# A gated short-convolution layer on one core: the adaLN sums divided anew between TensorE, VectorE and ScalarE, wider late groups, and products ordered by channel tile

## The chip, the core and the metric

The kernel runs on one core of one Trainium2 chip. A core has a TensorE (PE, the matmuls; its weight loads are listed apart as PEld), a VectorE (DVE), a ScalarE (ACT), a GpSimd (POOL) and a SyncE (SP) that here issues nearly all DMAs. Time is device microseconds (us) of one execution. Before the change the median of three runs is 928.99 us (926.72 to 929.95).

## The reference

One layer (DEPTH = 1, so the short convolution alone), 256 tokens of 2048 channels, all float32:

```python
h = rmsnorm(x, norm_g)                          # over the 2048 channels of a token
mod = silu(c) @ ada_w + ada_b                   # adaLN: one vector, 2048 -> 3 * 2048
shift, scale, gate = split(mod, 3)
h = h * (1 + scale) + shift
b_gate, c_gate, v, g = split(h @ w_in, 4)       # w_in: 2048 x 16384
u = causal_depthwise_conv(c_gate * v, conv_w)   # 3 taps
y = (b_gate * u * silu(g)) @ w_out              # w_out: 4096 x 2048
out = rmsnorm(x + gate * y, final_g)
```

## The kernel before

**Products in three terms.** Each float32 operand is split into a rounded high part and a remainder. `split` makes them of a weight tile: ACT casts `raw` to `hi` (L320), DVE subtracts to get `lo` (L321). The activations are kept turned, channel by token, in `hT`: for each of the 16 tiles of 128 input channels ("plane" k) the high part `hh_` and the remainder `hl_`. `product` (L415) issues hi·hh, hi·hl and lo·hh, each a matmul of 128x128 by 128x256.

**First half of the channels (`mm_s`).** A chunk is 512 channels of one quarter of `w_in`; 4 chunks by 4 quarters are kept as 16 accumulators `acc`. adaLN's shift and scale become known group by group of planes (`ADA = [2] * 8`: eight groups of two), and a product can use a plane only when its group is done. So `plan` walks through the 16 accumulators several times: `part` multiplies the planes k0 to k1 that are there by then, into a PSUM bank, and `keep` adds it to `acc` (L436, L438) or the bank is seeded from `acc` (L448). `plan` has figures of its own for what each step takes (`VPIECE`, `ALAG`) and puts the DMAs of adaLN's weights (`ada_piece`, L384, two DMAs for each tile `at`) between the parts. 24 products (two planes) come of 512 KB of `w_in`.

**adaLN's sums.** For a group, DVE accumulates silu(c)[k] times a row block of `ada_w` into `gv` (L395, L397): 16 row tiles, each 512 wide (256 of shift, 256 of scale). That leaves 128 partial sums, one per partition. `ada_done` turns `gv` on PE (L404, 4 transposes into PSUM `tp_g`), ACT sums each of the four blocks (L406, with an accumulator read), and `modulate` adds the biases on DVE (L305 to L307), writes `hh_` on ACT (L310), then shift and remainder on DVE (L311, L314). The first group has no time to wait: its 16 row tiles `at0` are the first thing loaded after x; DVE takes 13 of them (L344, L346), PE takes tiles 7, 11 and 15 directly as matmuls with silu(c) as the moving column (`sum0`, L333), and at the end PE adds DVE's partial sums by a column of ones. Between these, `idle` issues transposes into an unused bank (L236).

**Second half (`mm_b`).** Here all planes are there: banks of 256 channels, all 16 planes, per channel tile 8 planes times 3 terms in a row. The gate's part of adaLN (`gate_sums`, tiles `at_g` of 512 KB, four groups of 512) has the lowest priority; each group ends with matmuls by ones (`ps_gate`, L538).

**Last product (`mm_o`).** `w_out` in four column blocks, then gate, residual and the last rmsnorm.

**What sets the order.** Up to the first group's end the order on each engine is the order of the code (`in_order`). After that the framework's scheduler orders each engine's instructions by its own model; `later(GIVE)` lets adaLN's sums go behind other work. Every engine runs its list strictly in that order. Buffers: `raw` 3, `hi` 3, `lo` 3, `at` 4, PSUM `mm` 3, PSUM `sm` 2.

Of the kernel before, what the change touches and what calls it, by code (L numbers as in the profile page):

```python
# [13 lines left out]
P = 128  # L14
# [10 lines left out]
CT = 4  # L25
NCH = 4
NS = CT * NCH
ADA = [2] * 8
# [12 lines left out]
VPIECE = 1.5  # L41
# [5 lines left out]
ALAG = 9.0  # L47
# [4 lines left out]
def plan():  # L52
# [10 lines left out]
    def ada():  # L63
        nonlocal load, dve
        k0, nk, i = pieces.pop(0)
        steps.append(("ada", k0, nk, i))
        load = max(load, dve - AAHEAD) + ALOAD
        dve = max(dve, load + 2.0) + VPIECE
        if i == 4 * nk - 1:
            ready.extend([dve + ALAG] * nk)  # L70

# [46 lines left out]
def short_conv_layer(ctx: ExitStack, tc: tile.TileContext, x, c, norm_g, ada_w, ada_b, w_in, conv_w, w_out, final_g, out):  # L118
# [6 lines left out]
    const = ctx.enter_context(tc.tile_pool(name="const", bufs=1))  # L125
    adap = ctx.enter_context(tc.tile_pool(name="adap", bufs=2))
# [59 lines left out]
    IDLE = (16, 30, 24, 14, 14, 6)  # L186
# [58 lines left out]
    gT = vec[:, 0:16]  # L245
    b_shift = vec[:, 16:32]
    b_scale1 = const.tile([P, KT], F32, tag="bsc", name="b_scale1")
# [17 lines left out]
    nc.vector.tensor_scalar_add(b_scale1, vec[:, 32:48], 1.0)  # L265
# [11 lines left out]
    def turn_x(k0, k1, vector=False):  # L277
# [8 lines left out]
        for i in range(0, k1 - k0, 2):  # L286
# [4 lines left out]
            nc.scalar.copy(xs[k0 // CT][:, k0 % CT + i : k0 % CT + i + 2, :], tp)  # L291

    shift = const.tile([P, KT], F32, tag="shift", name="shift")
    scale = const.tile([P, KT], F32, tag="scale", name="scale")

    def modulate(k0, nk, sums):

        ks = slice(k0, k0 + nk)
        if nk == 1:
            nc.vector.tensor_scalar(  # L300
                out=scale[:, ks], in0=sums[1], scalar1=b_scale1[:, ks], scalar2=gT[:, ks], op0=ALU.add, op1=ALU.mult
            )
            nc.scalar.activation(shift[:, ks], sums[0], AF.Identity, bias=b_shift[:, ks])
        else:
            nc.vector.tensor_tensor(out=scale[:, ks], in0=sums[1], in1=b_scale1[:, ks], op=ALU.add)  # L305
            nc.vector.tensor_tensor(out=scale[:, ks], in0=scale[:, ks], in1=gT[:, ks], op=ALU.mult)
            nc.vector.tensor_tensor(out=shift[:, ks], in0=sums[0], in1=b_shift[:, ks], op=ALU.add)  # L307
        for k in range(k0, k0 + nk):
            hf = xs[k // CT][:, k % CT, :]
            nc.scalar.activation(hh_[:, k], hf, AF.Identity, bias=shift[:, k : k + 1], scale=scale[:, k : k + 1])  # L310
            nc.vector.tensor_scalar(  # L311
                out=hf, in0=hf, scalar1=scale[:, k : k + 1], scalar2=shift[:, k : k + 1], op0=ALU.mult, op1=ALU.add
# [3 lines left out]
    def split(raw, n):  # L316

        hi = wpool.tile([P, SLOT], F32R, tag="hi", name="hi", bufs=3)
        lo = wpool.tile([P, SLOT], F32R, tag="lo", name="lo", bufs=3)
        nc.scalar.copy(hi[:, :n], raw[:, :n])  # L320
        nc.vector.tensor_tensor(out=lo[:, :n], in0=raw[:, :n], in1=hi[:, :n].bitcast(F32), op=ALU.subtract)  # L321
        return hi, lo


    ON_PE = (7, 11, 15)
    sums0 = psum.tile([P, 512], F32, tag="sm", name="sum0", bufs=2)
    gv0 = adap.tile([P, 2, 2 * P], F32, tag="gv", name="gv0")[:, :, 0 : NK0 * P]
    turn_x(0, 4)

    def sum0(k, rows, col):  # L330

        for o in range(2 * NK0):
            nc.tensor.matmul(  # L333
                sums0[:, o : o + 1], rows[:, o // NK0, (o % NK0) * P : (o % NK0 + 1) * P], col,
                start=k == ON_PE[0] and o == 0, stop=k is None, skip_group_check=True,
            )

    for k in range(KT):
        c_k = silu_c[:, k : k + 1]
        if k in ON_PE:  # L340
            idle(IDLE[2 + ON_PE.index(k)])
            sum0(k, first_ada[k], c_k)
        elif k == 0:
            nc.vector.tensor_scalar_mul(gv0, first_ada[k], c_k)  # L344
        else:
            nc.vector.scalar_tensor_tensor(out=gv0, in0=first_ada[k], scalar=c_k, in1=gv0, op0=ALU.mult, op1=ALU.add)  # L346
    sum0(None, gv0, ones[:, 0:1])
    pieces0 = [split(raw0[:, 0 : CT * P], CT * P)]
    modulate(0, NK0, (sums0[:, 0:NK0], sums0[:, NK0 : 2 * NK0]))
    idle(IDLE[-1])  # L350
    pinned.close()
    with behind(ended):
        for k in range(1, NK0):
            pieces0.append(split(raw0[:, k * CT * P : (k + 1) * CT * P], CT * P))
# [345 lines left out]
```

## Time and profile before

| | |
|---|---|
| median of three runs | 928.99 us |
| the profiled execution's own time | 927.38 us |
| its span, first to last instruction | 925.6 us |
| first product of the trunk | 26.32 us |
| `mm_s` / `mm_b` / `mm_o` begin | 26.3 / 393.9 / 742.9 us |
| PE busy in the span | 906.1 us (98%) |
| DVE / ACT busy | 613.8 us (66%) / 472.9 us (51%) |
| DMA | 227.66 MB, mean 246 GB/s |

"Start" times are from the span's first instruction. A matmul's end is modelled, so the distance between starts tells PE's rate, not the length of one. A few matmul records are missing from the trace. In a row of stretches, the number in parentheses behind an engine is its count of instructions, PEclk is the granted share of TensorE's clock.

### The profile page before, as it was taken

To read this page: it belongs to the slowest core of one execution; us is meant where nothing else is said; L and a number is where in the kernel's file an instruction comes from. 1 tells how busy PE (TensorE), PEld (TensorE's weight loads), DVE (VectorE), ACT (ScalarE), POOL (GpSimd) and SP (SyncE) were. 2 spreads that over 40 slices of the span, in tenths; PEclk is the share of its full clock that TensorE was granted. 3 is DMA by queue.
4 is the path that set the end of the run, shared out by engine and by line. 5 is a ranking of instruction groups with operands and counts; after the bars stand their busy time and mean duration, and the time that the engine had idled before them with its cause. 6 is when DMAs were issued, how large, how long until landed. Compare 5 with 4: busy or idle time off the path is not lost.

```text
span 925.6 us, 16468 instructions
## 1 busy us (share of the span) xinstructions
PE 906.1 (98%) x7119; PEld 871.4 (94%) x7119; DVE 613.8 (66%) x604; ACT 472.9 (51%) x465; POOL 0.7 (0%) x6
## 2 busy tenths in 40 slices
PE   6999999999999999999999999999999999999996
PEld 6999999999999999999999999999999988888885
DVE  5889988897585799875554455445554554545882
ACT  3787866765557756644334433443334433444333
POOL 0000000000000000000000000000000000000000
PEclk9999999999999999999999999999999999999999
DMA  9999999999885689776656665666556685565542
GB/s 314 362 365 354 369 367 350 338 364 350 273 293 164 221 294 356 238 233 201 203 184 190 200 202 183 191 200 201 183 183 197 206 324 184 183 203 203 182 137 91
DMA packets 163753, 227.66 MB, mean 246 GB/s; under 512 B 5680, under 2 KB 104160, under 8 KB 163296
## 3 DMA queue, kind: packets, MB, share of 16 engines
q1 hardware_dynamic: 163440, 226.51, 73.4%
q8 instruction: 56, 0.92, 0.4%
q10 hardware_dynamic: 240, 0.09, 0.0%
q14 instruction: 17, 0.14, 0.0%
HBM read 224.49 MB, written 2.10 MB: 245 GB/s over the span
## 4 chain that ended last, share of the span: by engine, by line
PE 88%; DMA 5%; DVE 3%; ACT 1%; issue 1%; SPq 0%; ACTq 0%; DVEq 0%
PE mm_b L415 38%; PE mm_s L415 31%; PE mm_o L601 6%; PE mm_o L599 6%; PE mm_o L600 6%; DMA at<-in_ada_w_dram 2%; DMA raw_s<-in_sc_w_in_dram 2%; DVE gv L397 1%; DVE lo L321 1%; ACT hi L320 1%; DMA x<-in_x_dram 1%; PE ps_gate L538 0%; PE sum L333 0%; ACT x L281 0%; ACT x L285 0%
## 5 line engine op out<-in xcount | busy, mean ns | idle before, releaser
L415 PE MATMUL mm_s<-hT,hi 128*128 128x256 f32 x2048 | 355.0, 279 | 0.4 <-ACT hT L310 0.3
L415 PE MATMUL mm_b<-hT,hi 128*128 128x256 f32 x2048 | 348.8, 276 | 0.0
L415 PEld LDWEIGHTS mm_s<-hT,hi 128*128 128x128 f32 x2048 | 310.9, 189 | 1.4 <-ACT hT L310 0.7
L415 PEld LDWEIGHTS mm_b<-hT,hi 128*128 128x128 f32 x2048 | 308.7, 188 | 0.2 <-issue 0.2
L415 PE MATMUL mm_s<-hT,lo 128*128 128x256 f32 x1024 | 285.0, 279 | 4.6 <-DVE lo L321 4.6
L415 PE MATMUL mm_b<-hT,lo 128*128 128x256 f32 x1024 | 282.6, 276 | 0.0
L321 DVE TENSOR_TENSOR lo<-raw,hi 128x2048 fp32r<-128x2048 f32 (+1 forms) x66 | 148.1, 2244 | 134.9 <-ACT hi L320 134.9
L320 ACT CAST hi<-raw 128x2048 fp32r<-128x2048 f32 (+1 forms) x66 | 123.7, 1875 | 208.4 <-PE mm_b L415 150.1
L415 PEld LDWEIGHTS mm_s<-hT,lo 128*128 128x128 f32 x1024 | 192.3, 188 | 5.4 <-DVE lo L321 5.4
L415 PEld LDWEIGHTS mm_b<-hT,lo 128*128 128x128 f32 x1024 | 192.2, 188 | 0.2 <-issue 0.2
L321 DVE TENSOR_TENSOR lo<-raw_s,hi 128x2048 fp32r<-128x2048 f32 (+1 forms) x80 | 147.9, 1849 | 43.9 <-ACT hi L320 43.2
L320 ACT CAST hi<-raw_s 128x2048 fp32r<-128x2048 f32 (+1 forms) x80 | 124.7, 1558 | 69.6 <-PE mm_s L415 57.8
L321 DVE TENSOR_TENSOR lo<-raw_o,hi 128x2048 fp32r<-128x2048 f32 x32 | 73.3, 2291 | 65.8 <-ACT hi L320 65.8
L320 ACT CAST hi<-raw_o 128x2048 fp32r<-128x2048 f32 x32 | 61.3, 1915 | 107.0 <-PE mm_o L601 89.7
L600 PE MATMUL mm_o<-lo,y 128*128 128x512 f32 x256 | 99.7, 391 | 0.0
L599 PE MATMUL mm_o<-hi,y 128*128 128x512 f32 x256 | 99.3, 389 | 0.0
L601 PE MATMUL mm_o<-hi,y 128*128 128x512 f32 x256 | 99.3, 389 | 0.0
L397 DVE SCALAR_TENSOR_TENSOR gv<-at,silu_c,gv 128x512 f32<-128x512 f32 x105 | 78.6, 750 | 5.8 <-DMA at<-in_ada_w_dram 4.4
L436 ACT COPY acc<-mm_s 128x1024 f32<-128x1024 f32 x54 | 54.4, 1010 | 32.3 <-PE mm_s L415 32.3
L600 PEld LDWEIGHTS mm_o<-lo,y 128*128 128x128 f32 x256 | 48.1, 188 | 10.2 <-issue 0.2
L601 PEld LDWEIGHTS mm_o<-hi,y 128*128 128x128 f32 x256 | 48.1, 188 | 10.2 <-issue 0.2
L599 PEld LDWEIGHTS mm_o<-hi,y 128*128 128x128 f32 x256 | 48.1, 188 | 9.9
(94 smaller groups left out, 375.2 us busy)
## 6 DMA issues: line engine op xcount, KB each, us to landing
raw<-in_sc_w_in_dram SPq DMA_DIRECT2D x64, 1024.0 KB, 5.6
raw_s<-in_sc_w_in_dram SPq DMA_DIRECT2D x47, 1024.0 KB, 7.7
raw_o<-in_sc_w_out_dram SPq DMA_DIRECT2D x32, 1024.0 KB, 5.1
at<-in_ada_w_dram SPq DMA_DIRECT2D x114, 256.0 KB, 7.2
raw_s<-in_sc_w_in_dram SPq DMA_DIRECT2D x33, 512.0 KB, 5.7
at_g<-in_ada_w_dram SPq DMA_DIRECT2D x32, 512.0 KB, 7.7
at<-in_ada_w_dram SPq DMA_DIRECT2D x6, 512.0 KB, 8.3
x<-in_x_dram SPq DMA_DIRECT2D x4, 512.0 KB, 6.2
```

Of the source, the lines that this page charges most:

```text
L320: nc.scalar.copy(hi[:, :n], raw[:, :n])
L321: nc.vector.tensor_tensor(out=lo[:, :n], in0=raw[:, :n], in1=hi[:, :n].bitcast(F32), op=ALU.subtract)
L397: nc.vector.scalar_tensor_tensor(out=gv, in0=at4[:, i], scalar=c_k, in1=gv, op0=ALU.mult, op1=ALU.add)
L415: mm = last_mm[0] = nc.tensor.matmul(dst, w, h[:, k], start=begins and left, stop=ends, skip_group_check=True)
L436: nc.scalar.copy(acc[ch, q], bank)
L599: nc.tensor.matmul(po, yh, hi[:, o], start=opens, stop=False, skip_group_check=True)
L600: nc.tensor.matmul(po, yh, lo[:, o], start=False, stop=False, skip_group_check=True)
L601: nc.tensor.matmul(po, yl, hi[:, o], start=False, stop=ct == NCT - 1, skip_group_check=True)
```

## The change

- **Groups.** `ADA = [2, 2, 2, 2, 4, 4]`: the last eight planes come in two groups of four. A row tile of such a group is 1024 wide; `at` has 3 buffers instead of 4, `gv` is twice as large. `VPIECE` depends on the width, `ALAG` is 11 instead of 9, so `plan` orders parts and adaLN pieces differently.
- **First sums.** PE takes row tiles 3, 7, 10, 11, 13 and the shift half of 15; DVE takes the other ten and the scale half of 15; the final column of ones is applied half by half. The `idle` counts change (`IDLE_AT`, `IDLE_END`; 104 idle transposes become 79).
- **Biases in one step.** norm_g is no longer multiplied into `scale`: it scales the turned x when it leaves PSUM (four ACT instructions of 256 in place of two of 512, per `turn_x`). Shift and scale lie in one tile `mod`, so that one addition does what three did.
- **Cast ahead.** `split` is cut in two; the high part of the first chunk's second plane is cast before the first `modulate`.
- **Later sums.** `ada_done`: DVE's `reduce_sum` over the four transposed blocks in place of four ACT sums; twice for a group of four.
- **Chunks by channel tile.** `chunk_products` takes all the planes of a weight tile and runs channel tile by channel tile, each over all these planes, instead of plane by plane. The first part keeps its order (`late`).
- **Gate.** Two groups of 1024 instead of four of 512: 32 sums of 1024 instead of 64 of 512.

```diff
-ADA = [2] * 8
+ADA = [2, 2, 2, 2, 4, 4]
-VPIECE = 1.5
+VPIECE = {2: 1.5, 4: 1.28}
-ALAG = 9.0
+ALAG = 11.0
...
-    IDLE = (16, 30, 24, 14, 14, 6)
+    IDLE = (16, 30)
+    IDLE_AT = {3: 0, 7: 6, 10: 15, 11: 0, 13: 3, 15: 4}
+    IDLE_END = 5
...
-            nc.scalar.copy(xs[k0 // CT][:, k0 % CT + i : k0 % CT + i + 2, :], tp)
+                k = k0 + i + j
+                nc.scalar.activation(xs[k // CT][:, k % CT], tp[:, j], AF.Copy, scale=gT[:, k : k + 1])
...
-            nc.vector.tensor_tensor(out=scale[:, ks], in0=sums[1], in1=b_scale1[:, ks], op=ALU.add)
-            nc.vector.tensor_tensor(out=scale[:, ks], in0=scale[:, ks], in1=gT[:, ks], op=ALU.mult)
-            nc.vector.tensor_tensor(out=shift[:, ks], in0=sums[0], in1=b_shift[:, ks], op=ALU.add)
+        sums = sums.rearrange("p (s k) -> p s k", s=2)
+        nc.vector.tensor_tensor(out=mod[:, :, ks], in0=sums, in1=bias[:, :, ks], op=ALU.add)
...
-    ON_PE = (7, 11, 15)
...
+        at, gv = first_ada[k], gv0
+        if k in IDLE_AT:
+            idle(IDLE_AT[k])
+            sum0(k, at, c_k, (0,) if k == KT - 1 else (0, 1))
+            if k < KT - 1:
+                continue
+            at, gv = at[:, 1], gv0[:, 1]
...
-    sum0(None, gv0, ones[:, 0:1])
+    for half in range(2):
+        sum0(None, gv0, ones[:, 0:1], (half,))
     pieces0 = [split(raw0[:, 0 : CT * P], CT * P)]
-    modulate(0, NK0, (sums0[:, 0:NK0], sums0[:, NK0 : 2 * NK0]))
-    idle(IDLE[-1])
+    hi0 = [split_hi(raw0[:, k * CT * P : (k + 1) * CT * P], CT * P) for k in range(1, NK0)]
+    modulate(0, NK0, sums0[:, 0 : 2 * NK0])
+    idle(IDLE_END)
...
-        at = adap.tile([P, ASLOT], F32, tag="at", name="at", bufs=4)
+        at = adap.tile([P, ASLOT], F32, tag="at", name="at", bufs=3)
...
-        for o in range(2 * nk):
-            nc.tensor.transpose(tp[:, o, :], gv[:, o // nk, (o % nk) * P : (o % nk + 1) * P], ident)
-        for o in range(2 * nk):
-            nc.scalar.activation(tp[:, o, :], tp[:, o, :], AF.Copy, accum_out=gs[:, o : o + 1])
+        for h in range(nk // 2):
+            tp = psum.tile([P, 4, P], F32, tag="sm", name="tp_g", bufs=2)
+            for i in range(4):
+                o = h * 4 + i
+                nc.tensor.transpose(tp[:, i, :], gv[:, o // nk, (o % nk) * P : (o % nk + 1) * P], ident)
+            nc.vector.reduce_sum(gs[:, h * 4 : h * 4 + 4], tp, axis=mybir.AxisListType.X)
...
-        terms = [(m, i) for i in (0, 2, 1) for m in range(CT)] if late else [(m, i) for m in range(CT) for i in range(3)]
+        terms = [(m, j, i) for m in range(CT) for j in range(n) for i in range(3)]
...
-            for i in range(sk):
-                chunk_products(bank, hi, lo, i * CT * P, s0 + i, k0, k1, seed)
+            chunk_products(bank, [(hi, lo, i * CT * P, s0 + i) for i in range(sk)], first, k1, seed)
...
-    gate_todo = [(dc, j) for dc in range(4) for j in range(0, KT, 2)]
+    gate_todo = [(h, j) for h in range(2) for j in range(KT)]
```

Three places where instructions move. The first is ScalarE's list at the end of the first group's sums (`xs` is the turned x, `raw_111` or `raw_112` the first chunk's weights, `raw_s` the second chunk's, `hT` the first two planes). Before:

```order
L291 COPY xs_196<-tp_x 128x512 x2
L320 CAST hi<-raw_111 128x512
L310 ACTIVATE hT<-xs_196,shift,scale 128x256 x2
L320 CAST hi<-raw_111 128x512
L320 CAST hi<-raw_s 128x1024
```

And now:

```order
L295 ACTIVATE xs_196<-tp_x,vec 128x256 x4
L314 CAST hi<-raw_112 128x512 x2
L314 CAST hi<-raw_s 128x1024
L306 ACTIVATE hT<-xs_196,mod 128x256 x2
L284 ACTIVATE x_84<-x_84,rstd 128x512
```

Both planes now stand behind two more casts, that of the first chunk's second plane and that of the second chunk, which is 1024 wide.

The second place is SyncE's list of DMAs from the second chunk's weights on (`at`: adaLN's tiles, each DMA a half of one, 256 KB). Before:

```order
L458 DMA raw_s<-in_sc_w_in_dram 128x2x512 x2
L384 DMA at<-in_ada_w_dram 128x2x256 x8
L458 DMA raw_s<-in_sc_w_in_dram 128x2x512 x2
L384 DMA at<-in_ada_w_dram 128x2x256 x4
L458 DMA raw_s<-in_sc_w_in_dram 128x2x512
```

And now:

```order
L471 DMA raw_s<-in_sc_w_in_dram 128x2x512 x2
L393 DMA at<-in_ada_w_dram 128x2x256 x6
L471 DMA raw_s<-in_sc_w_in_dram 128x2x512 x2
L393 DMA at<-in_ada_w_dram 128x2x256 x2
L471 DMA raw_s<-in_sc_w_in_dram 128x2x512
```

With one buffer less, two halves fewer run ahead at first, and `plan` brings the pieces later: ahead of the weights of product number 577 (counted from the trunk's first) the list has 52 halves before and 44 now, and the same 12,800 KB of `raw_s`, these weights included.

The third place is PE's last interruptions of the trunk's products. Before, behind product 2400 of the 3072 of `mm_s`:

```order
L415 MATMUL mm_s<-hT,hi 128x256 x2
L415 MATMUL mm_s<-hT,lo 128x256
L538 MATMUL ps_gate<-gacc,ones 128x512 x2
L415 MATMUL mm_s<-hT,hi 128x256 x2
L415 MATMUL mm_s<-hT,lo 128x256
```

And now behind product 4881, in `mm_b`:

```order
L425 MATMUL mm_b<-hT,hi 128x256 x2
L425 MATMUL mm_b<-hT,lo 128x256
L549 MATMUL ps_gate<-gacc,ones 128x512
L425 MATMUL mm_b<-hT,hi 128x256 x2
L549 MATMUL ps_gate<-gacc,ones 128x512
```

The gate's matmuls have left `mm_s`. The transposes `tp_g` stand behind products 301, 528, 626, 1248 and 1800 now, the last two as eight in a row; before they stood at eleven places between 264 and 1848. So from product 1800 to product 4881 nothing else runs on PE.

112 lines of the change are left out of this document (54 added, 58 removed).

## The prediction, made before the changed kernel was run

> **What bounds the kernel now.** First the page's busy line, then PE's waits:
>
> ```profile
> PE 906.1 (98%) x7119; PEld 871.4 (94%) x7119; DVE 613.8 (66%) x604; ACT 472.9 (51%) x465; POOL 0.7 (0%) x6
> PE mm_s L415 <- DVE lo L321: 4.6, 4, 1.9
> PE sum L333 <- DMA at<-in_ada_w_dram: 1.2, 1, 1.2
> ```
>
> PE is the bound nearly everywhere. After the trunk's start it waits four times, 4.6 us in all, each time for `lo`. So what can be won: an earlier start, these waits, and PE's own rate. The view by stretches shows the rest:
>
> ```profile
> 26.30:103.50 77.20, 72.60 (x615) 71.56 (x615) 72.27 (x96) 61.32 (x83) 0.00 (x0) 0.98 1.06 362
> 103.50:180.00 76.50, 76.43 (x661) 76.43 (x662) 66.13 (x80) 53.67 (x66) 0.00 (x0) 1.00 1.05 355
> ...
> 258.00:314.00 56.00, 56.00 (x478) 1.00 0.71 229
> 322.00:378.00 56.00, 56.00 (x497) 1.00 0.92 323
> 500.00:556.00 56.00, 56.00 (x496) 1.00 0.62 194
> ```
>
> (First two rows: PE, PEld, DVE, ACT, POOL, clock, DMA share, GB/s; the others PE alone.) Up to 103.5 three things are full at once: PE 72.60 of 77.20, DVE 72.27, the DMA engines over 1.0 at 362 GB/s. Later PE is never idle, yet not always equally fast: at full clock it issues 478 products in one 56 us and 497 in another, 117.2 against 112.7 ns each. The slow rate holds for whole stretches:
>
> ```profile
> 125.70:157.00 31.30, 31.22 (x264) 1.00 1.05 356
> 171.00:179.50 8.50, 8.50 (x73) 1.00 0.99 318
> 251.00:315.90 64.90, 64.90 (x552) 1.00 0.70 227
> ...
> 250.62 0.49 PE L404 MATMUL tp_g<-ident,gv 128*128 128x128 f32 x3
> ```
>
> Each begins right behind transposes `tp_g`, the longest behind those of the last row, and ends at an interruption by transposes or `ps_gate` that leaves PE fast again. 104.7 us at 19 in 497 slower is **4.0 us**, the largest loss after 103.5. I read it as two steady rates, one of which PE falls into when products restart: of the seven restarts behind `tp_g` from 125 us on, four were slow; the two behind `ps_gate` before `mm_o` were fast.
>
> **The change, part by part.** All against the profiled execution: 927.38 us, a span of 925.6 and 1.8 around it; the median, 928.99, is 1.6 above that.
>
> *First sums and biases.* What ended last:
>
> ```profile
> 16.00 7.12 DMA at<-in_ada_w_dram
> 23.17 1.96 PE sum L333 x16
> 25.15 0.17 DVE scale L305
> 25.67 0.61 ACT hT L310
> ```
>
> The end is set by the landing of row tile 15, not by DVE, so the sums that PE takes from DVE give nothing. Behind the landing PE has half of 8 records less (0.5 us), and one addition instead of three saves 25.67 − 25.15 less one step, 0.3. That would start the planes at 24.9. But the order puts a 1024-wide cast ahead of them:
>
> ```profile
> DMA to landing us min/median/max: 5.7/5.7/5.7
> 19.78 1.80 SPq L458 DMA_DIRECT2D raw_s<-in_sc_w_in_dram  x2
> 27.18 1.04 ACT L320 CAST hi<-raw_s 128x1024 fp32r<-128x1024 f32 x1
> 26.32 1.90 PE mm_s L415 x8
> ```
>
> (The first row is of the DMA issued at 19.78.) These weights land at 19.78 + 5.7 = 25.5; the cast takes 1.04, so the planes start near 26.6 and the first product, 0.65 behind as now, near 27.25: **0.9 us later**, not 0.8 earlier. By itself this costs the end nothing, since PE waits in front of this product anyhow:
>
> ```profile
> 34.32 0.39 PE L415 MATMUL mm_s<-hT,lo 128*128 128x256 f32 x1 [0.83 <-DVE lo L321]
> ```
>
> PE's clock adds to it:
>
> ```profile
> 22.07:25.49 3.42, 2.32 (x21) 2.32 (x22) 2.58 (x7) 0.62 (x1) 0.00 (x0) 1.00 1.05 368
> 25.49:28.90 3.41, 3.11 (x16) 2.72 (x14) 2.61 (x9) 3.23 (x6) 0.00 (x0) 0.50 1.08 352
> ```
>
> After a stretch with PE busy 2.32 of 3.42 us the granted clock was 0.50 for 3.41 us. With the start at 27.25, PE has some 1.7 us of work in 25.49 to 28.90, so a second half-speed stretch may follow; it costs up to 1.7 us, of which I count 0.7 because DVE's `lo` is late there anyhow. The Trainium skill, "TensorE: Matmul & The Clock Gate", Part 1, has the clock halved after an idle window of about 3.4 us. By that rule no second stretch follows and the 0.7 falls away; the rows here are stricter, since 2.32 us of work did not keep the clock up.
>
> *Up to product 577* (103.57 now), three sums. **DMA:** 8 halves of 256 KB fewer lie ahead of its weights, 2.1 MB, at 362 GB/s 5.8 us. **DVE** is what ended last there:
>
> ```profile
> 101.23 2.30 DVE lo L321
> 103.53 0.04 issue
> 103.57 0.50 PE mm_s L415 x2
> ...
> L397 DVE SCALAR_TENSOR_TENSOR gv<-at,silu_c,gv 128x512 f32<-128x512 f32 x50 | 37.5, 750 | 3.1 <-DMA at<-in_ada_w_dram 2.3
> L321 DVE TENSOR_TENSOR lo<-raw_s,hi 128x1024 fp32r<-128x1024 f32 x17 | 20.8, 1221 | 1.7 <-ACT hi L320 1.7
> L321 DVE TENSOR_TENSOR lo<-raw_s,hi 128x2048 fp32r<-128x2048 f32 x4 | 9.1, 2284 | 0.0
> L314 DVE TENSOR_TENSOR hT<-xs,hT 128x256 fp32r<-128x256 f32 x6 | 2.5, 422 | 0.1
> L311 DVE TENSOR_SCALAR xs<-xs,scale,shift 128x256 f32<-128x256 f32 x6 | 2.5, 410 | 0.7 <-ACT hT L310 0.7
> L306 DVE TENSOR_TENSOR scale<-scale,vec 128x2 f32<-128x2 f32 x2 | 0.3, 158 | 0.0
> ```
>
> By the new order DVE has, up to that `lo`, 43 of the 512-wide sums instead of 50 and one fewer that opens a group (−5.3, −0.5), two planes fewer (−1.7), 19 and 3 `lo` for 17 and 4 (+0.2), 2 bias steps for 6 (−0.6), and two sums of `tp_g`. Such a sum of 512 elements in PSUM isn't in the trace; the nearest row is a two-input step of 512 that reads PSUM:
>
> ```profile
> L660 DVE TENSOR_TENSOR big<-mm_o,gate 128x512 f32<-128x512 f32 x6 | 3.9, 685 | 2.4 <-PE mm_o L601 2.4
> L406 ACT ACTIVATE tp_g<-tp_g 128x128 f32<-128x128 f32 x28 | 7.4, 263 | 0.7 <-PE tp_g L404 0.3
> L406 ACT ACTIVATION_READ_ACCUMULATOR tp_g<-tp_g 128x1 f32 x28 | 5.4, 192 | 0.0
> L260 DVE SCALAR_TENSOR_TENSOR junk<-x 128x1024 f32<-128x1024 f32 x2 | 2.5, 1225 | 7.8 <-DMA x<-in_x_dram 7.8
> ```
>
> I take 0.69; between 0.16 (the bias step) and 1.22 (a 1024-wide step) it is 0.3 to 2.4 for both. Sum: −6.5, so DVE comes to 103.57 − 6.5 + 0.9 = 98.0. The skill, "VectorE: DVE Perf Modes", Rules for kernel authors, advises against a `tensor_reduce` on a hot path as DVE's slowest step; by it this edit would be a loss, but here four ACT sums with their reads cost 1.8 us per group. **PE** alone: 27.25 + 576 × 0.113 + 32 transposes × 0.1 + 1.5 for the half clock (0.8 up to 28.9 and the 0.7) = 97.0. So product 577 could start at 98, 5.5 us earlier.
>
> From that I take **2.3 us** for the new order by channel tile. In a four-plane chunk whose last two planes are new, the seventh product already needs the first of them, where it was the 25th. The first later group:
>
> ```profile
> 61.62 0.60 PE L404 MATMUL tp_g<-ident,gv 128*128 128x128 f32 x4
> 73.65 0.42 DVE L314 TENSOR_TENSOR hT<-xs,hT 128x256 fp32r<-128x256 f32 x1
> ```
>
> Transposes to last plane took 12.4 us, with sums and casts between. DVE's sum and one bias step take 1.5 us out of it; what is left is 8 to 11 us of queueing behind 2.3 us `lo` and 1.9 us casts. The sum is also a new wait of DVE: it stands in its list until PE has done the transposes, and the bias step and the next `lo` queue behind it, so up to 2 us of DVE idle can come of PE being behind. The new order leaves 41 products, 4.7 us, between transposes (behind 301) and first use (343), then six products to the next plane; for the second group 54 (528 to 583). That gives waits of 1 to 4 and of 0 to 1 us; part of the first is absorbed because DVE is the later one at 577. Front: **−3.2 us** (0 to −5.5).
>
> *Behind product 577* nothing waits on DMA or DVE now, and the 1024-wide sums (1225 against 2 × 750) and the two gate groups take some 17 us off DVE (64 sums instead of 128; 48 if the wide one cost only 0.75, nothing at 1.5), and PE hides all of it. Four `ps_gate` move along PE's list, no fewer. ACT's scaled copies of x lie in its slack (61.32 of 77.20). So there only the rate counts. Restarts behind 626, 1248 and 1800 decide over 622, 552 and 3081 products, at 4.5 ns each 2.8, 2.5 and 13.9 us if slow. In the likeliest course the last is fast and one earlier one slow half the time: 4.0 − 1.4 = **−2.6 us**.
>
> Sum: 927.4 − 3.2 − 2.6 = **921.6 us**; its own range 918 to 926.
>
> **The rivals.**
>
> *A slow last restart (27%): slower.* From product 1800 on nothing interrupts PE for 3081 products, into `mm_b`, where before `ps_gate` came after 552 products and left it fast. If those eight transposes leave PE slow, 13.9 us go: 921.6 + 13.9 = **935.5**. It decides as soon as the slow rate lasts over some 1,300 products (5.8 us, all that was won). For it: four of seven restarts behind `tp_g` were slow. Against it: the new order of products is that of `mm_b`, where no slow stretch exists (496 in 56 us), though its one restart there, behind `ps_gate`, proves little.
>
> *The order by channel tile ends the slow rate (18%).* In `mm_s` each three products go to another part of the bank, in `mm_b` 24 go to one. If that switching is what the slow rate needs, all 4.0 us come back and no restart matters: 927.4 − 3.2 − 4.0 = **920.2**.
>
> *The front gives nothing (18%).* The planes' waits, the later start and the half clock eat the whole 5.5: 927.4 − 2.6 = **924.8**, up to 927 with both earlier restarts slow.
>
> **How the numbers follow.** Forecast 37%, rivals 27, 18, 18. About 0.3%, 2.8 us, is what a measurement here can tell from no change; against the median that is below 926.2 and above 931.8. Faster: nine tenths of the forecast and of the second rival, and half of the third: 0.59. Slower: most of the first rival, 0.23. The rest, 0.18, is the same. The range must reach into the slow case: 918 to 935.5.
>
> **What would show it.** Start: first product near 27.2, with a granted clock of 0.50 from 25.49 and perhaps again. Front: product 577 near 100, PE's waits there for `hT` rather than `lo`. Rate: 56 us stretches in 260 to 580 with 497 products (fast) or 478 (slow) are the whole question of 921 or 935. Wrong would be: waits of PE behind 110 us, or a front slower than 103.6.

## The result, and the profile after

The changed kernel takes 941.03 us, the median of four runs (937.49 to 942.97), against 929.34 of the kernel before: a ratio of 1.0129, with a 95% interval of 1.0109 to 1.0149. It is slower by 12 us where I had forecast 7 us faster. (Runs more than 1.5% above the fastest of their kernel stay out of the ratios, here and below.) The profiled run took 942.86 us, 15.5 more than the profiled run of before. Where these lie, by the first instruction of each stage:

| | before | after | difference |
|---|---|---|---|
| first product | 26.32 | 34.26 | +7.9 |
| `mm_b` begins | 393.86 | 402.29 | +8.4, so `mm_s` +0.5 |
| `mm_o` begins | 742.91 | 757.78 | +14.9, so `mm_b` +6.4 |
| end of the span | 925.6 | 941.1 | +15.5, so `mm_o` +0.6 |

So two places carry nearly all of it: the start, and `mm_b`. All 6144 products of the two halves are in each of the traces, so they can be numbered. The page's busy line and PE's waits of the changed kernel look harmless:

```profile
PE 922.8 (98%) x7114; PEld 888.0 (94%) x7114; DVE 601.9 (64%) x523; ACT 474.9 (50%) x424; POOL 0.7 (0%) x6
PE mm_s L425 <- DVE lo L319: 2.3, 2, 2.0
PE mm_s L425 <- ACT hi L314: 0.8, 1, 0.8
PE mm_s L425 <- DVE hT L310: 0.8, 1, 0.8
```

PE is busy for 16.7 us more, and waits less than before. The loss is work that takes longer. The view by stretches, cut at the clock's own steps of 3.41 us (PE, PEld, DVE, ACT, POOL, granted clock, DMA share, GB/s), shows the first of the two:

```profile
9.88:13.29 3.41, 2.78 (x25) 2.54 (x23) 2.21 (x8) 0.82 (x2) 0.00 (x0) 1.00 1.09 354
13.29:16.70 3.41, 1.59 (x9) 0.98 (x10) 2.07 (x4) 2.13 (x5) 0.00 (x0) 1.00 1.10 348
16.70:20.12 3.42, 3.42 (x20) 3.42 (x18) 2.68 (x4) 0.47 (x1) 0.00 (x0) 0.50 1.10 350
20.12:23.53 3.41, 3.41 (x18) 3.41 (x18) 2.85 (x5) 0.62 (x1) 0.00 (x0) 0.50 1.04 350
...
30.36:33.77 3.41, 3.41 (x18) 3.41 (x17) 0.16 (x1) 1.51 (x3) 0.00 (x0) 0.50 0.00 1
33.77:37.18 3.41, 3.41 (x17) 3.23 (x16) 2.87 (x6) 3.41 (x7) 0.00 (x0) 0.50 0.00 0
```

The granted clock is 0.50 for six steps, 20.5 us, where up to 50 us it was so for one before (and for two more from 81.6 us on, where before had none). In those six PE has no idle time at all, and from 30.4 us the DMA engines stand still. DVE's and ACT's timelines say who waits for whom (in brackets the idle time ahead and what ended it):

```profile
23.18 0.48 DVE L353 SCALAR_TENSOR_TENSOR gv<-at,silu_c,gv 128x256 f32<-128x256 f32 x1 [0.45 <-DMA at<-in_ada_w_dram]
33.35 0.16 DVE L303 TENSOR_TENSOR mod<-sum,vec 128x4 f32<-128x4 f32 x1 [9.09 <-PE sum L336]
33.61 1.09 ACT L306 ACTIVATE hT<-xs,mod 128x256 fp32r<-128x256 f32 x2 [0.92 <-DVE mod L303]
```

DVE waits 0.45 us for its part of the last row tile and starts on it at 23.18, when it has landed; the bias step then idles 9.09 us until PE has worked through its one-column sums. PE's sums, which had ended 2 us behind the landing, now end 10 us behind it and set the end of the stage. The second place is the rate, again PE alone in stretches of 56 us:

```profile
200.00:256.00 56.00, 56.00 (x497) 1.00 0.96 337
500.00:556.00 56.00, 56.00 (x497) 1.00 0.62 194
620.00:676.00 56.00, 56.00 (x478) 1.00 0.59 186
```

From 194 to 607 us PE is fast, behind the last transposes too. It falls into the slow rate behind the gate's matmuls at 607 and stays there up to `mm_o`: 1261 products at 4.45 ns more, 5.6 us of the 6.4 that `mm_b` lost.

### The profile page after: what moved, and what is told of

Same layout as the page of the kernel before. It is cut to its first block, busy times and chain, and to the rows that moved or that the text cites. A ratio compares the mean times of both kernels' runs of the same rounds, so it can differ in the third digit from the quotient of the medians.

```text
span 941.1 us, 16323 instructions
## 1 busy us (share of the span) xinstructions
PE 922.8 (98%) x7114; PEld 888.0 (94%) x7114; DVE 601.9 (64%) x523; ACT 474.9 (50%) x424; POOL 0.7 (0%) x6
## 4 chain that ended last, share of the span: by engine, by line
PE 91%; DMA 5%; DVE 2%; ACT 1%; issue 1%; SPq 0%; ACTq 0%; DVEq 0%
PE mm_b L425 38%; PE mm_s L425 32%; PE mm_o L612 6%; PE mm_o L611 6%; PE mm_o L610 6%; DMA raw_s<-in_sc_w_in_dram 2%; DMA at<-in_ada_w_dram 2%; PE sum L336 1%; DMA x<-in_x_dram 1%; DVE lo L319 1%; PE tp_idle L240 1%; DVE gv L406 1%; ACT hi L314 1%; PE ps_gate L549 0%; PE tp_g L415 0%
## 5 line engine op out<-in xcount | busy, mean ns | idle before, releaser
L425 PE MATMUL mm_s<-hT,hi 128*128 128x256 f32 x2048 | 358.6, 280 | 1.6 <-ACT hi L314 0.8
L425 PE MATMUL mm_b<-hT,hi 128*128 128x256 f32 x2048 | 354.3, 278 | 0.0
L406 DVE SCALAR_TENSOR_TENSOR gv<-at,silu_c,gv 128x512 f32<-128x512 f32 (+1 forms) x75 | 72.0, 961 | 8.1 <-DMA at<-in_ada_w_dram 7.4
L450 ACT COPY acc<-mm_s 128x1024 f32<-128x1024 f32 x59 | 59.6, 1011 | 24.3 <-PE mm_s L425 24.3
L611 PEld LDWEIGHTS mm_o<-lo,y 128*128 128x128 f32 x256 | 48.0, 188 | 10.2 <-issue 0.2
L612 PEld LDWEIGHTS mm_o<-hi,y 128*128 128x128 f32 x256 | 48.0, 188 | 10.2 <-issue 0.2
```

The costliest lines, as they stand in the source:

```text
L406: nc.vector.scalar_tensor_tensor(out=gv, in0=at4[:, i], scalar=c_k, in1=gv, op0=ALU.mult, op1=ALU.add)
L425: mm = last_mm[0] = nc.tensor.matmul(dst, w, h[:, k], start=begins and left, stop=ends, skip_group_check=True)
L450: nc.scalar.copy(acc[ch, q], bank)
L611: nc.tensor.matmul(po, yh, lo[:, o], start=False, stop=False, skip_group_check=True)
L612: nc.tensor.matmul(po, yl, hi[:, o], start=False, stop=ct == NCT - 1, skip_group_check=True)
```

## The experiments

Sixteen experiments with thirteen kernels, in four groups, each group with runs of the kernel before on the same chip. Times are medians, ratios have their 95% interval; where a kernel has two times I give its runs. An edit moves more than its own lines: the scheduler puts the transposes of the third later group behind product 626 in the changed kernel and in b2, behind 576 in a1, behind 583 in c3 and behind 768 in a2, a3, b1, b3 and b4; those behind 1248 and 1800 stay in all of these.

**1. The turned x without its waits (a1).** Both ScalarE copies stand behind all four transposes:

```diff
             for j in range(2):
                 for t, xn in enumerate((x0, x1)):
                     nc.tensor.transpose(...)
+            for j in range(2):
                 k = k0 + i + j
                 nc.scalar.activation(xs[k // CT][:, k % CT], tp[:, j], AF.Copy, ...)
```

> The changed kernel with one move: in turn_x the two scaled copies out of PSUM come behind all four transposes of the pair instead of one behind each two. In the changed kernel TensorE waited for these copies between 14.5 and 16.4 us and its clock was 0.50 from 16.7 to 37.2 us. Theory 'waits': these waits cost it the clock, so here the transposes run back to back, the clock stays at 1.00 to about 25 us, the first product starts near 27 us and the kernel takes about 933 us. Theory 'sums': the one-column matmuls of the first sums with few idle transposes cannot hold the clock whatever stands before them; then the clock is lost again before 22 us, the first product starts at 32 to 34 us and the time stays at 938 to 943 us.

936.97 us (934.08 to 940.20), ratio 1.0096 (1.0063 to 1.0129). PE no longer waits for `xs` between the transposes, yet the clock is 0.50 for the same 20.5 us, from 14.87, and the first product starts at 33.46. So these waits alone are not the cause.

**2. The first sums as before (a2).** Row tiles 7, 11 and 15 on PE again, 52 idle transposes between them, one column of ones for both halves:

```diff
-    IDLE_AT = {3: 0, 7: 6, 10: 15, 11: 0, 13: 3, 15: 4}
-    IDLE_END = 5
+    IDLE_AT = {7: 24, 11: 14, 15: 14}
+    IDLE_END = 6
...
```

> The changed kernel with the first sums as before: TensorE takes row tiles 7, 11 and 15 alone, behind 24, 14 and 14 idle transposes, VectorE takes the rest, one column of ones at the end; the copies of turn_x stay one behind each two transposes. Theory 'sums': the 52 idle transposes bring the clock back or keep it, first product near 27 us, about 933 us. Theory 'waits': the clock is lost at about 16 us all the same; 24 idle transposes at half speed take 5.1 us, they may win it back one step later, so first product at 28 to 31 us, 934 to 938 us.

951.47 us (951.06 to 952.30), ratio 1.0254 (1.0237 to 1.0271): the start is mended, and the kernel is slower than ever. Its stretches:

```profile
11.83:15.24 3.41, 1.30 (x9) 0.68 (x8) 2.10 (x7) 2.11 (x4) 0.00 (x0) 1.00 1.09 347
15.24:18.66 3.42, 2.85 (x14) 2.46 (x14) 3.13 (x5) 1.37 (x3) 0.00 (x0) 0.50 1.10 349
18.66:22.07 3.41, 3.41 (x33) 3.41 (x32) 2.62 (x5) 0.00 (x0) 0.00 (x0) 1.00 1.11 357
...
130.00:186.00 56.00, 56.00 (x478) 1.00 0.99 345
500.00:556.00 56.00, 56.00 (x478) 1.00 0.60 186
640.00:696.00 56.00, 56.00 (x478) 1.00 0.60 188
```

The clock falls here as well, behind a step in which PE waits for x and is busy 1.30 us; but the next step, with 12 transposes of 128 columns and no one-column sum, wins it back, and the first product starts at 28.0. The price comes later: 117.8 ns per product from 129 us to `mm_o`, over some 5370 products, 23.9 us. A part of that is the rival that I had given 27%: the restart behind product 1800 is slow, and 3081 products pay 13.7 us.

**3. Plane by plane (a3), and the first sums alone (a4).** a3 is the changed kernel with the order of the chunks undone; a4 is the kernel before with the new first sums only.

```diff
-        terms = [(m, j, i) for m in range(CT) for j in range(n) for i in range(3)]
+        terms = [(m, j, i) for j in range(n) for m in range(CT) for i in range(3)]
```

> The changed kernel with the products of a chunk plane by plane, as before. Theory of the prediction: by channel tile the seventh product of a chunk needs a new plane, by plane the 25th; so the waits for hT behind product 336 and 576 go and 2.3 us are won, 938 to 939 us. Rival: these waits are hidden behind other lateness (first product still at 34 us), less than 1 us changes but for the slow rate, whose stretches may fall otherwise (up to 6 us either way). If only the order by planes has the slow rate, the trace shows more slow stretches than the changed kernel.

> The kernel before with the new first sums alone (TensorE takes tiles 3, 7, 10, 11, 13 and half of 15, idle transposes cut from 104 to 79). Theory 'sums': the clock is lost before 22 us, the first product starts 4 to 8 us later than 26.3, the time is 931 to 936 us. Theory 'waits': the copies of turn_x are those of before, the clock holds to 25 us, the first product starts within 1 us of 26.3 and the time is within 3 us of before.

a3 took 934.57, 949.13, 952.05 and 956.56 us. The profiled run, the first, is slow in three stretches before 131 us, and then has 113.3 ns per product from there to 599 us and 117.8 behind the gate's matmuls; so the slow rate is not bound to either order of products. a4: 932.30 us (ten runs, 927.34 to 940.31), ratio 1.0045 (1.0014 to 1.0076). In its profiled run, the slowest, the new sums alone bring back the long half clock:

```profile
11.14:14.55 3.41, 1.58 (x13) 1.15 (x12) 2.20 (x8) 1.63 (x3) 0.00 (x0) 1.00 1.10 348
14.55:17.97 3.42, 3.42 (x18) 3.07 (x16) 2.35 (x4) 1.17 (x2) 0.00 (x0) 0.50 1.10 348
17.97:21.38 3.41, 3.41 (x19) 3.41 (x18) 2.65 (x4) 0.00 (x0) 0.00 (x0) 0.50 1.09 356
```

The first product starts at 33.24. Its runs spread over 13 us, and four of the ten are as short as the kernel before, so this loss seems a matter of the run; only one of them has a profile.

**4. More idle transposes (b1, run again as c4).** 50 ahead of x instead of 30, and 63 instead of 28 among PE's row tiles.

```diff
-    IDLE = (16, 30)
-    IDLE_AT = {3: 0, 7: 6, 10: 15, 11: 0, 13: 3, 15: 4}
+    IDLE = (16, 50)
+    IDLE_AT = {3: 8, 7: 16, 10: 15, 11: 8, 13: 8, 15: 8}
```

> The changed kernel with more idle transposes: 50 instead of 30 ahead of the first transposed x, and 8, 16, 15, 8, 8, 8 instead of 0, 6, 15, 0, 3, 4 ahead of the six row tiles that PE takes (40 + 20 more in all: 63 against 28 behind the x). Theory 'the clock follows the wide work': one-column matmuls count for next to nothing, the share of 128-column transposes in a window of 3.41 us decides; so the granted clock is 1.0 from 10 to 25 us, with at most one window of 0.50, the first product starts near 27.5 (34.26 in the changed kernel) and the time falls by about 6 us to 935. Rival 'PE simply has too much to do at the start': 55 more transposes of 0.11 us (0.2 at half clock) make it later, the first product starts behind 38 and the time grows by 4 us or more, to 945.

> The kernel with more idle transposes everywhere, once more and unchanged: its profiled run took 938.7 us with 113.3 ns per product from 135 to 603 us, its three other runs 951.5 to 956.7. Theory 'the same program draws either rate': a run near 953 shows 117.8 ns from some restart ahead of 300 us up to the gate's matmuls, over 3000 products or more, 14 to 18 us; a run near 939 shows 113.3 as before. Rival 'those runs were slow for another reason': a run near 953 with 113.3 ns and a longer wait or a lower clock elsewhere.

b1: 938.72, 953.67, 956.65 and 951.51 us; c4: 936.10. In both profiles the clock is 1.00 from 13 us to behind 100: some 34 instructions per step instead of 18, 10 to 16 of them one-column sums, the rest transposes. So the clock seems to follow the wide work, and not PE's busy time; section 9 counts it. But both were too much of a cure: at full clock PE is now the bound through its idle transposes, the first product starts at 32.3 and 30.1, and the expected 27.5 was wrong. Both profiled runs are fast from 135 us up to the gate's matmuls; b1's other three were not profiled.

**5. The gate's groups (b2), and with the first sums (b3).** Four gate groups of 512 as before; their matmuls stand behind products 4114, 4882, 5650 and in `mm_o`.

```diff
-    gate_todo = [(h, j) for h in range(2) for j in range(KT)]
+    gate_todo = [(dc, j) for dc in range(4) for j in range(0, KT, 2)]
...
```

> The changed kernel with the gate's sums as before (four groups of 512; their matmuls stand behind products 4114, 4882, 5650 and in mm_o, each pair of passes alone, instead of two groups with two products between their matmuls behind 4881). Theory 'the rate is set at each restart': the restart behind a single gate matmul is fast, as it was in every kernel so far that had one, so no product of mm_b takes 117.8 ns behind 4114; the slow 148 us behind the old place shorten by 5.6 us and the time falls to about 935.5, if the start is as slow as in the changed kernel. Rival 'mm_b is slow late in the run whatever stands there': no change, 941.

> The changed kernel with the first sums and the gate's sums as before (the earlier run with the first sums alone undone took 951.5, with 117.8 ns per product from 129 us to 766). Theory 'set at each restart': slow from 129 us on up to product 4114 at most, then the gate matmuls at 4114, 4882 and 5650 leave it fast over 2030 products, 9 us less: about 942. Rival 'the slow rate belongs to this run of the kernel': slow to the end, 951.

b2: 945.16 us (940.25 to 945.34), ratio 1.0155 (1.0128 to 1.0181); b3: 952.14 us (950.66 to 954.30), ratio 1.0250 (1.0233 to 1.0268). Both theories failed, and in b3 the rival, slow to the end, came out. Ahead of and behind the first gate matmul at 519 us in b2:

```profile
440.00:496.00 56.00, 56.00 (x497) 1.00 0.63 197
530.00:586.00 56.00, 56.00 (x477) 1.00 0.77 245
```

A single gate matmul turned PE slow, and the two after it left it so; in b3 three of them left a slow PE slow. "Fast behind `ps_gate`" is no rule.

**6. A spare matmul as a cure (b4).** On a2, one 512-column matmul more for each later group, into a bank that nobody reads.

```diff
+        spare = psum.tile([P, 512], F32, tag="sm", name="spare", bufs=2)
+        if nk == 4:
+            nc.tensor.matmul(spare, ones, gv[:, 0, :], start=True, stop=True)
...
```

> The changed kernel with the first sums as before, and a spare matmul of 512 columns (ones times adaLN's partial sums, into a bank that nobody reads) in each of the five later groups; they stand behind products 302, 528, 768, 1277 and 1823, so the last two follow the last two groups' transposes by some 25 products. Each costs about 1 us. Theory 'a restart behind a wide fp32 matmul is fast, one behind transposes is a lottery': products 1277 to 1800 and 1823 to 4881 take 113.3 ns instead of 117.8, 16 us less, for 5 us of spare matmuls: about 940.5 instead of 951.5. Rival 'any restart draws anew': the spare ones are slow in about half the places and the time is anywhere between 940 and 956.

951.54 us (950.20 to 953.40), ratio 1.0238 (1.0221 to 1.0254): no cure. In its profiled run the transposes behind 1248 and 1800 left PE fast, and the spare matmuls some 25 products later turned it slow both times, the second time up to `mm_o`.

**7. Eight groups of two again (c1), and plane by plane (c2).** First sums, groups, four buffers `at` and gate as before; left are scaled copies, one bias step, the cast ahead, the sums on VectorE, and in c1 the order by channel tile.

```diff
-ADA = [2, 2, 2, 2, 4, 4]
+ADA = [2] * 8
-        at = adap.tile([P, ASLOT], F32, tag="at", name="at", bufs=3)
+        at = adap.tile([P, ASLOT], F32, tag="at", name="at", bufs=4)
...
```

> The changed kernel with the first sums as before, adaLN's later groups eight of two planes again, four buffers at, and the gate as before; what is left of the change: scaled copies and one bias step, the cast ahead, later sums on VectorE, chunks by channel tile. Theory 'the missing fourth buffer idles the DMA engines': with the first sums alone undone their share was 0.59 in 28 to 32 us, 0.80 in 44 to 48 and 0.88 in 80 to 90, because SyncE's list stood at a raw_s behind a late lo, where before it was 1.03 to 1.09 throughout; so here the share is at least 1.03 in every 4 us from 36 to 90 and product 552 starts at 100 or earlier (98.5 before, about 102.8 with the first sums alone undone). Rival 'the order by channel tile makes the products wait for the new planes': the share stays full but product 552 starts behind 102. The time depends on the rate that the restarts draw as well: 925 to 931 with few slow ones, up to 945 with 117.8 ns from the last transposes on.

> The same with the chunks plane by plane, so that only the scaled copies, the one bias step, the cast ahead and the later sums on VectorE are left of the change. If the order by channel tile costs something, product 577 starts earlier than in the run with eight groups by channel tile, by up to 2.3 us (my figure in the prediction); if the buffer was all, both are alike within 0.5 us. VectorE's work up to there is less than before by the bias steps alone and more by the sums, so about as before: product 577 at 102 to 104 (103.6 before). Time 925 to 931, if the rate is drawn as before.

c1: 940.73 us (938.00 to 943.99), ratio 1.0135 (1.0102 to 1.0167). c2: 929.98 us (928.42 to 931.13), ratio 1.0012 (1.0003 to 1.0022). They differ in one line, the order, and in 11 us. The buffer theory fell: with four buffers the DMA share in c1 is still 0.92 in 36 to 40 and 0.99 in 44 to 48, and product 552 starts at 106.8, not at 100. What the order does there, PE in c1 and then in c2, waits for the first new planes:

```profile
71.14 0.39 PE L422 MATMUL mm_s<-hT,lo 128*128 128x256 f32 x1 [1.97 <-DVE lo L319]
75.58 0.58 PE L422 MATMUL mm_s<-hT,lo 128*128 128x256 f32 x1 [2.51 <-DVE lo L319]
77.62 0.58 PE L422 MATMUL mm_s<-hT,hi 128*128 128x256 f32 x1 [0.60 <-DVE hT L310]
...
70.53 0.39 PE L422 MATMUL mm_s<-hT,lo 128*128 128x256 f32 x1 [1.73 <-DVE lo L319]
75.57 0.39 PE L422 MATMUL mm_s<-hT,lo 128*128 128x256 f32 x1 [1.92 <-DVE lo L319]
```

Two waits of some 2 us in both. Between them c2 has 24 products of old planes to do. In c1 a channel tile has six of them, because the seventh product needs a new plane; PE's list then turns to the next chunk, whose `lo` isn't there yet. And then the clock, c1's two stretches and one of c2:

```profile
69.62:73.04 3.42, 1.59 (x7) 1.02 (x7) 3.38 (x5) 3.18 (x4) 0.00 (x0) 1.00 1.09 358
73.04:76.45 3.41, 0.90 (x5) 0.87 (x5) 3.41 (x5) 0.08 (x1) 0.00 (x0) 0.50 1.04 381
...
69.62:73.04 3.42, 2.51 (x22) 2.51 (x23) 2.82 (x5) 2.88 (x3) 0.00 (x0) 1.00 1.09 350
```

In c1 it is 0.50 for 10.2 us, in c2 not once behind 20 us. The product that the prediction has at 103.57 starts at 104.4 in c2, just behind the 102 to 104 expected, and at 111.6 in c1.

**8. The order alone (d2), first sums and order undone together (d1).** d2 is the kernel before with the new order and nothing else; d1 the changed kernel without both.

> The kernel before with the chunks by channel tile and nothing else. Theory 'the order costs the front': PE waits 2 to 3 us for hT or lo at the first new group, the clock falls to 0.50 for one to three windows of 3.41 us behind it, product 552 starts at 103 to 106 instead of 98.5, and the time grows by 5 to 11 us to 934 to 940. Rival 'the order costs only together with the other parts': within 2.8 us of the kernel before.

> The changed kernel with the first sums and the order plane by plane as before; the wide groups, three buffers at, the gate in two groups, later sums on VectorE, one bias step and the cast ahead are left. Theory 'first sums and order are the whole loss': first product at 28, product 768 at 126 or earlier (128.8 in the kernel with the first sums alone undone), mm_b from 394 if the restarts are fast; the time is 926 to 932 then, or up to 948 if the rate is slow from 130 us on. Rival 'three buffers and wide groups cost the front as much': product 768 at 129 or later all the same.

d2: 928.84 us (ten runs, 926.87 to 934.40), ratio 1.0000 (0.9982 to 1.0019). Its front behaves as expected, with the clock at 0.50 from 72.3 for two steps and product 552 at 103.9 instead of 98.5; yet the time doesn't change. In the profiled run `mm_b` begins only 2.3 us later, mostly because the 552 products behind 1848 were slow before, for 2.5 us, and are fast here; and single runs vary by as much. So the order's price in the median is not a constant: nothing here, 11 us in c1. d1: 950.98 us (948.14 to 951.77), ratio 1.0231 (1.0206 to 1.0255), with nearly all products behind 124 us slow. Its front goes by the rival: product 768 starts at 129.5, 4.4 us later than before. Of this 3.2 us are the first product, at 29.53 and not at 28, behind two steps at 0.50 from 14.9 us; the way from there to 768 takes 1.2 us longer. Without the 23.9 us of the slow rate its profiled run would be at 927.7, which is worked out and not measured.

**9. One program, two rates (c3, run again as d3 and d4).** The changed kernel with 50 idle transposes ahead of x, nothing else.

```diff
-    IDLE = (16, 30)
+    IDLE = (16, 50)
```

> The changed kernel with 50 instead of 30 idle transposes ahead of the first turned x, and nothing else: the wait for x is bridged, the sums are carried by as few transposes as in the change. Theory 'the clock is lost in the wait for x, and the sums with few transposes then cannot win it back': with the wait bridged the clock is 1.0 up to 22 us at least, PE finishes the sums at most one window at 0.50 later, the first product starts at 27.5 to 30 (34.3 in the changed kernel, 32.3 with more idle transposes everywhere at full clock). Rival 'the sums themselves lose it': 0.50 comes within two windows behind the x, for 10 us or more, and the first product starts at 32 or later.

> Another look at the changed kernel with 50 idle transposes ahead of x, unchanged. Theory 'one program draws either rate': a run of 933 to 938 has 113.3 ns per product from 112 or 190 us to 600, one of 955 to 959 has 117.8 ns there, over some 4200 products, 19 us. Rival: a run of 955 to 959 with 113.3 ns there and its 20 us elsewhere.

> The same kernel and the same question: 933 to 938 with 113.3 ns from 190 us to 600, or 955 to 959 with 117.8 ns.

c3's runs: 936.03, 956.40, 937.35, 933.33 and 958.53 us; the ratio without the two long ones is 1.0074 (1.0047 to 1.0101). In the profile of the first run neither theory held: the clock is at 0.50 for two steps from 17.6 us and for two more from 27.8, and the first product starts at 30.25. d3 took 932.87 us and d4 958.69: the same program, 26 us apart, both profiled. With first products at 27.70 and 35.79 they lie on both sides of it, so bridging the wait for x is no sure cure. PE at the start, d3 and then d4:

```profile
16.42 0.44 PE L293 MATMUL tp_x<-ident,x 128*128 128x128 f32 x2 [0.71 <-ACT xs L295]
20.68 1.84 PE L336 MATMUL sum<-silu_c,at 128*128 128x1 f32 x16
24.40 1.03 PE L336 MATMUL sum<-ones,gv 128*128 128x1 f32 x8
27.70 1.22 PE L425 MATMUL mm_s<-hT,hi 128*128 128x256 f32 x4 [1.14 <-ACT hT L306]
...
18.89 0.44 PE L293 MATMUL tp_x<-ident,x 128*128 128x128 f32 x2 [0.71 <-ACT xs L295]
25.88 3.41 PE L336 MATMUL sum<-silu_c,at 128*128 128x1 f32 x16
32.99 1.85 PE L336 MATMUL sum<-ones,gv 128*128 128x1 f32 x8
35.79 1.22 PE L425 MATMUL mm_s<-hT,hi 128*128 128x256 f32 x4
```

Sixteen sums take 1.84 us in the one and 3.41 in the other. Their clock, two steps of d3 and two of d4:

```profile
15.12:18.53 3.41, 2.70 (x24) 2.46 (x24) 2.36 (x4) 1.31 (x3) 0.00 (x0) 1.00 1.09 347
18.53:21.95 3.42, 3.42 (x34) 3.42 (x33) 2.63 (x5) 0.00 (x0) 0.00 (x0) 1.00 1.09 358
...
16.80:20.22 3.42, 2.15 (x18) 1.75 (x17) 2.65 (x4) 1.79 (x4) 0.00 (x0) 1.00 1.10 351
20.22:23.63 3.41, 3.41 (x19) 3.41 (x18) 2.82 (x5) 0.62 (x1) 0.00 (x0) 0.50 1.05 360
```

The two waits for `xs` are the same in both; in d4 they fall into one step of the clock with less wide work, and the sums behind them cannot win the clock back for 20.5 us. That it is the wide work and not the busy time shows best in two pairs of steps, of d3 and then of b3:

```profile
21.95:25.36 3.41, 3.41 (x34) 3.41 (x34) 1.69 (x3) 1.16 (x2) 0.00 (x0) 1.00 0.94 314
25.36:28.77 3.41, 2.27 (x11) 1.87 (x11) 1.21 (x4) 2.75 (x6) 0.00 (x0) 0.50 1.06 361
...
13.75:17.16 3.41, 1.93 (x14) 1.51 (x15) 3.11 (x5) 1.93 (x5) 0.00 (x0) 1.00 1.10 348
17.16:20.58 3.42, 3.42 (x34) 3.42 (x33) 2.63 (x4) 0.00 (x0) 0.00 (x0) 1.00 1.09 351
```

In d3 PE is busy for the whole step, with 24 one-column sums and 8 transposes starting in it, and loses the clock. In b3 it is busy 1.93 us, with 14 transposes, and keeps it. I counted the transposes that start in each step ahead of the first product, from 7 us on, in all 18 profiles: behind 10 or fewer the next step was at 0.50, all 38 times; behind 14 or more it was at 1.00, all 54 times; behind 11 to 13 it went either way, 12 times. Then the rate in 300 to 356 and 500 to 556 us, d3 and d4:

```profile
300.00:356.00 56.00, 56.00 (x497) 1.00 0.80 269
500.00:556.00 56.00, 56.00 (x497) 1.00 0.62 190
...
300.00:356.00 56.00, 56.00 (x478) 1.00 0.88 292
500.00:556.00 56.00, 56.00 (x477) 1.00 0.61 188
```

From 194 to 623 us some 3630 products are slow in d4, 16.1 us, and the start costs 8.1: 24.2 of the 25.8 us. So two thirds of d4's excess are the slow rate behind the last two transposes, and one third is the half clock of the start. That the long times of a3 and b1 are the same slow rate is argued from their size (a3: 15 to 22 us above its profiled run), not shown.

## Why the prediction was wrong, step by step

Up to the product that the prediction has at 103.57 the front was to win 3.2 us; it lost 9.9. From there to the end 2.6 were to be won; 5.6 were lost. Together that is the 21.3 us between the forecast of 921.6 and the profiled 942.86.

**The start** (0.9 us later by ScalarE's order, 0.7 for a second half-clock step). The order was read rightly: where the clock held long enough, in d3, the planes followed the 1024-wide cast, the clock fell at 25.36 for two steps, and the first product started at 27.70 against my 27.25. The step that failed is the clock's term: 0.7 us, measured about 6.6 (34.26 less the 27.70 of d3). I had taken it for one more step of 3.41 us, and had given the sums that PE takes over no price, as if they stayed hidden behind the landing. They are what ends last once the clock is at 0.50: 52 records of one-column sums at 0.21 us instead of 0.12, with the transposes between them slowed as well. The row that should have warned me was in the prediction: PE busy 2.32 of 3.42 us, most of it one-column sums, and then half clock. I read it as too little work; a2, a4, b1 and the count of section 9 show that it was the wrong kind. The Trainium skill, "TensorE: Matmul & The Clock Gate", Part 1, gives the full clock back after a window of some 3.4 us in which PE is busy; the rows here disagree, since PE was busy 3.41 of 3.41 us in step after step at 0.50. The same part calls the window free-running, and with that the runs agree: the steps of d3 and d4 lie differently against the same instructions.

**The front** (−3.2 us). The product that the prediction calls 577 and has at 103.57 is, counted in the trace, the 579th, the first behind 576 that needs the new `lo`; I mean the same one here. It starts at 113.5 us, which is the front slower than 103.6 that I had named as a sign of being wrong. Of the 9.9 us the start is 7.9; the way from the first product takes 79.2 us against 77.3 before, and 78.3 in d3, with a good start. DVE's work did fall, and the sum of `tp_g` takes 0.68 us where I took 0.69. But between 36 and 104 us neither the DMA engines nor DVE are as full as they were, before and then after (and SyncE's longest waits from 15 to 110 us):

```profile
36.00:104.00 68.00, 64.18 (x556) 63.33 (x555) 62.80 (x82) 52.15 (x71) 0.00 (x0) 1.00 1.06 362
36.00:104.00 68.00, 64.99 (x527) 64.38 (x527) 56.61 (x70) 49.31 (x59) 0.00 (x0) 0.94 0.96 316
...
SPq L458 <- DVE lo L321: 14.2, 15, 1.8
SPq L471 <- DVE lo L319: 37.8, 21, 11.3
```

I had added up totals of three engines; what sets the end is a chain through all of them. SyncE's list stood 37.8 us instead of 14.2 at a `raw_s` that needs the buffer of a late `lo` (11.3 of it in the start), so the bytes saved bought no earlier landing. Two steps at 0.50 from 81.6 us, behind a wait of PE, add to it. Over the 18 profiles the way to this product grows with such steps: 76.2 to 78.5 us where none, or only the beginning of one, lies on it behind 40 us (eight profiles), 77.3 to 80.9 with one (six), 79.2 to 80.6 with two (three) and 83.7 with three (c1). Waits and lost clock come together there, so how much each takes stays open. The fourth buffer alone, in c1, is not enough; with it, groups of two and the old order, in c2, the way is 76.2, and with three buffers, wide groups and the old order, in d1, 78.0. The 2.3 us for the order by channel tile were right in kind and too small: it cost 7.2 us between c2 and c1, with the clock that its waits lose.

**The rate** (−2.6 us). Two steady rates, up to 19 in 497 apart, were right, and behind product 1848 no profile changes its rate without an interruption. The likeliest course was right as far as I had followed it: the last transposes left PE fast and one earlier restart (behind 626) was slow. The step that failed is the restart behind the gate's matmuls: the sum has no term for the 1261 products behind them, because I took a restart behind `ps_gate` for a fast one, from two examples. They were slow and cost 5.6 us. The gate's pair with products between its matmuls was followed by the slow rate in all eleven profiles that have it in `mm_b`, seven times behind a fast one. Against the 4.0 us of before, the kernel now has 5.6 in `mm_b` and 2.8 behind product 626. Nor does each restart draw anew, as I had it: behind the eight transposes at 1800 twelve of thirteen profiles kept the rate that they had, and behind the gate's two matmuls in a row at 2400 PE was fast in all five that have them. But a single gate matmul at 5650 left PE fast before, in a4 and in d2 and turned it slow in c1 and c2.

**The rivals.** The slow last restart did not come in the changed kernel's profiled run, and its four runs lie within 5.5 us, but it is real and my price for it, 13.9 us, was right: 13.7 in a2, and it or worse in b3, d1 and d4. In four of thirteen profiles with that restart the products behind it were slow, so 27% was a fair chance. "Channel tile ends the slow rate" is refuted by the 622 products behind 626 in `mm_s` and by the rows after 620 us above. "The front gives nothing" had the start and the half clock in it, but the front lost 9.9 us where this rival let it lose nothing. None of the three gave the half clock of the start a price of its own, although a row of before showed it.

The kernel before stays the best: c2 and d2 come level with it and no version is faster. Why PE takes one rate or the other at a restart is not settled. Neither the kind of the matmul ahead nor the program alone decides it, and no run here moves the gate's pair alone back into `mm_s`.

## What to carry to other kernels

Before giving TensorE narrow matmuls to relieve another engine, count the wide columns in each 3.41 us, not its busy time, and keep enough of them behind every wait, since a lost clock turns an engine with slack into the bound. Where PE is the bound, look at its rate per instruction in long stretches and ask what each restart is worth: one that three thousand products follow was a 14 us bet here. Judge an edit to such a kernel by several profiles, because two runs of one program can differ by more than the edit.

## What the runs showed of the hardware

- The granted clock stayed at 0.50 for 20.5 us while PE showed no idle time, with one-column sums and 3 to 12 transposes of 128 columns starting in a step. Ahead of the first product 10 or fewer transposes in a step of 3.41 us were always followed by 0.50 and 14 or more always by 1.00 (92 steps of 18 profiles); in the 12 steps with 11 to 13 either came.
- At full clock products of 256 columns follow each other at 113.3 or 117.8 ns for hundreds of microseconds; one program took either in two runs (d3, d4).
- In the last product, `mm_o`, the slow rate was never seen, in any of the 18 profiles (nearly all its products of 512 columns follow at 226 to 228 ns), though gate matmuls interrupt it too.
